# A hybrid RWKV-7 and dilated-attention block: recurrence products with a block-diagonal state, y's gate factors made beside the norm, loads issued ahead, a third staging slot

## The chip, the core and the metric

The kernel runs on one core of one Trainium2 chip, in one launch. The metric is the device time of a run in microseconds (us). TensorE (PE) multiplies, VectorE (DVE), ScalarE (ACT) and GpSimd (POOL) do the element-wise work, SyncE (SP) issues most of the DMAs.

## The reference, cut to what matters

One layer over 1024 tokens with model width 1024, all in float32. The recurrence of 8 heads of 64 and the gated norm behind it are what the change rewrites.

```python
x = x + 0.5 * swiglu(rms_norm(x, ffn1_norm), ffn1_w_gate, ffn1_w_up, ffn1_w_down)   # d_ff 2816
z = rms_norm(x, mix_norm) @ w_in
z_rwkv, z_attn, z_gate = jnp.split(z, [RWKV_COLS, RWKV_COLS + ATTN_COLS], axis=-1)
y_rwkv = rwkv7_time_mix(z_rwkv, ...)
y_attn = dilated_attention_mix(z_attn, cos, sin, q_norm, k_norm)      # 3 groups of 4 heads, rms_norm and rope on q, k
g_rwkv, g_attn = jnp.split(jax.nn.sigmoid(z_gate), 2, axis=-1)
merged = g_rwkv * (y_rwkv @ w_br_rwkv) + g_attn * (y_attn @ w_br_attn)
x = x + merged @ w_out
x = x + 0.5 * swiglu(rms_norm(x, ffn2_norm), ffn2_w_gate, ffn2_w_up, ffn2_w_down)
x = x + jax.nn.sigmoid(rms_norm(x, ple_norm) @ ple_w_gate) * (p_i @ ple_w_proj)
...
# rwkv7_time_mix, per step t and head:
    sa = jnp.einsum('bhvk,bhk->bhv', state, -kk_t)
    state = state * w_t[:, :, None, :] + sa[..., None] * (kk_t * a_t)[:, :, None, :] + v_t[..., None] * k_t[:, :, None, :]
    y_t = jnp.einsum('bhvk,bhk->bhv', state, r_t)
...
    y = (y - mean) * lax.rsqrt(var + GN_EPS)
    y = y * gn_w + gn_b
    y = (y + bonus) * g            # bonus = sum(r k r_k) * v, g = sigmoid(gd) @ g2
```

## The kernel before, in words

The kernel is a chain of stages: FFN1 (0 to 800 us in the profiled execution, with the norm and the first gates behind it), the recurrence (800 to 1403), the attention (1403 to 1750), the merge of the two branches (1750 to 1840), the output product (to 1920), FFN2 (to 2640) and the last gated product. A large product is made of three fp32r matmuls on high and low halves (`mm3`, lines 265 to 267; tile `g` in the stages of interest). Weights are loaded into a ring `wst` of 128x1024 tiles and split by ACT (L249) and POOL (L250) into `wsp`, which `mm3` reads.

In the recurrence the work is cut into 8 units (4 pairs of heads, 2 halves of the sequence), each of 8 chunks of 64 tokens. Three streams, written as generators, run over the units one behind another: A and B prepare a unit (`zstage`, decays, the matrices of a chunk, a triangular solve), and C (`wkv_c`) runs the chunks of a unit, then norms y, gates it, transposes it (L1330) and writes it out. A fourth stream, F, the filler, holds large products that nothing near waits for: the rest of `w_in`, gates, the attention's q, k, v. `weave` fixes the order of all of it when the program is built: each stream yields pairs (busy, wait) in us, and the order is made of them. Afterwards each engine runs its own list strictly in order, so a matmul whose operand is late holds all matmuls behind it, filler too. Filler placed by a long `wait` is what covers a chain.

In a chunk, U = S·QR (L1255, two 64x64 products, one for each head), then DVE makes UV (L1259), then dS = BKn·UV (L1264, two products), then DVE makes the next S (L1265) with ACT's SP = S·decay (L1258). After the chunks of a unit, y's products (L1273, L1279, tile `psy`), then on DVE mean and variance (L1303 to L1315), an rsqrt of eleven small operations (L237 to L243), yc·rs (L1319), on POOL yc·gn_w, +gn_b, the bonus UV·bon and yc+bonus (L1320 to L1325), on DVE yc·gs (L1327, `gsl` is the gate tile loaded from DRAM), and the four transposes. Of the next unit the same queues carry `z`, `kk`, `BK` (L1029, L1031), the products t = QR·BK (L1056) and a matrix N (DVE L1186, read by PE L1192 and L1194).

In the attention, `qk_post` brings q and k of a group (rope, norm, transposes L1516), `attn_core` runs scores (L1576), softmax and output (L1619) over 8 blocks of a group. Three groups follow one another; their filler is the products of the later groups and of the branches (`branch_r`, L1699 loads its gate tiles).

## Time and profile before

| | us |
|---|---|
| median of 3 runs | 2728.99 (2728.43 to 2731.87) |
| profiled execution, time | 2728.36 |
| its span, first to last instruction | 2726.6 |
| PE busy | 2517.1 (92%) |
| DVE busy | 1615.6 (59%) |
| POOL busy | 1144.9 (42%) |
| ACT busy | 972.4 (36%) |
| mean granted clock of TensorE | 0.961 |

Busy time says how full an engine is over the whole span, and nothing of where the others wait for it. PE is the full one; its clock is the share of full speed that was granted while it ran. At a lower clock the same matmul takes longer and counts as longer busy time, so lost time has two forms: idle time of PE, and busy time at a low clock.

### The profile page before, as it was taken

The page shows a single profiled execution, that of the slowest core. Times are in us where ns is not written, and L with a number is a line of the kernel's source. Part 1 is how long each engine was busy: PE and PEld are TensorE (multiplying, and loading weights), DVE is VectorE, ACT ScalarE, POOL GpSimd, SP SyncE. Part 2 cuts the span into 40 slices and gives each one's busy share as a digit, 9 for nine tenths or more (in the row PEclk, how much of TensorE's full clock was granted, in tenths as well). Part 3 has the DMA queues.
Part 4 walks back from the last instruction along what each step waited for, and adds up shares of the span by engine and source line. Part 5 has one row for each costly group of instructions (what it writes and reads, how often), then busy time and mean ns, then how long its engine had stood idle before and what let it go on. Part 6 is the DMA issues. An engine that isn't in the chain of part 4 may idle for free.

```text
span 2726.6 us, 37039 instructions
## 1 busy us (share of the span) xinstructions
PE 2517.1 (92%) x14541; PEld 2037.5 (75%) x14541; DVE 1615.6 (59%) x2519; ACT 972.4 (36%) x1700; POOL 1144.9 (42%) x635
## 2 busy tenths in 40 slices
PE   6899999998999999889988998879889999989899
PEld 5688888777777666667977898658678888868677
DVE  5865556897715555554356326382676565688952
ACT  6433332334434333332224343421533333333541
POOL 2675655554424333332222203151466556553540
PEclk9899999999999999999999999999899999999999
DMA  5222222746333222222231101563032222373532
GB/s 187 93 93 68 88 78 93 263 139 224 117 117 90 53 66 60 56 64 61 74 115 44 63 24 50 174 197 124 31 108 93 79 91 93 125 257 98 177 124 93
DMA packets 272498, 289.18 MB, mean 106 GB/s; under 512 B 46282, under 2 KB 202540, under 8 KB 272068
## 3 DMA queue, kind: packets, MB, share of 16 engines
q1 hardware_dynamic: 264932, 274.59, 30.7%
q10 hardware_dynamic: 7392, 12.23, 1.3%
q8 instruction: 114, 1.87, 0.3%
q14 instruction: 60, 0.49, 0.1%
HBM read 222.64 MB, written 64.14 MB: 105 GB/s over the span
## 4 chain that ended last, share of the span: by engine, by line
PE 47%; DVE 14%; issue 3%; POOL 3%; DMA 2%; ACT 2%; SPq 0%; DVEq 0%; POOLq 0%; ACTq 0%
PE g L265 7%; PE g L267 6%; PE g L266 6%; PE dn L266 5%; PE dn L267 5%; PE dn L265 5%; PE tr L266 1%; PE tr L265 1%; PE tr L267 1%; POOL wsp L250 1%; PE t L1056 1%; PE s L1576 1%; DVE sub L1120 1%; PE pt L1598 1%; PE st L1264 1%
## 5 line engine op out<-in xcount | busy, mean ns | idle before, releaser
L250 POOL TENSOR_TENSOR wsp<-wr,wsp 128x1024 fp32r<-128x1024 f32 (+1 forms) x158 | 355.2, 2254 | 373.8 <-ACT wsp L249 309.0
L250 POOL TENSOR_TENSOR wsp<-wst,wsp 128x1024 fp32r<-128x1024 f32 x71 | 172.9, 2437 | 428.6 <-ACT wsp L249 375.8
L250 POOL TENSOR_TENSOR wsp<-ws,wsp 128x1024 fp32r<-128x1024 f32 x88 | 221.1, 2515 | 212.7 <-ACT wsp L249 210.2
L265 PE MATMUL g<-h,wsp 128*128 128x512 f32 x496 | 221.1, 446 | 15.2 <-DVE h L1715 13.7
L265 PE MATMUL g<-wsp,h 128*128 128x256 f32 (+1 forms) x664 | 217.7, 328 | 13.6 <-ACT raw L1428 10.8
L267 PE MATMUL g<-wsp,h 128*128 128x256 f32 (+1 forms) x664 | 208.2, 314 | 0.0
L266 PE MATMUL g<-wsp,h 128*128 128x256 f32 (+1 forms) x664 | 208.0, 313 | 0.0
L267 PE MATMUL g<-h,wsp 128*128 128x512 f32 x496 | 201.5, 406 | 0.0
L266 PE MATMUL g<-h,wsp 128*128 128x512 f32 x496 | 201.3, 406 | 0.0
L407 DVE TENSOR_TENSOR ws<-wr 128x512 f32<-128x512 f32 x56 | 86.4, 1552 | 161.5 <-POOL x L250 160.1
L249 ACT ACTIVATE wsp<-ws 128x1024 fp32r<-128x1024 f32 (+1 forms) x110 | 106.4, 968 | 202.2 <-PE dn L267 78.0
L249 ACT ACTIVATE wsp<-wr 128x1024 fp32r<-128x1024 f32 (+1 forms) x158 | 134.3, 853 | 121.7 <-PE g L267 46.8
L265 PEld LDWEIGHTS g<-wsp,h 128*128 128x128 f32 x664 | 138.8, 209 | 26.0 <-ACT raw L1428 11.4
L265 PE MATMUL dn<-wsp,h 128*128 128x512 f32 x360 | 143.5, 399 | 12.8 <-DVE x L792 8.8
L266 PE MATMUL dn<-wsp,h 128*128 128x512 f32 x360 | 142.8, 397 | 6.0 <-POOL wsp L250 6.0
L267 PE MATMUL dn<-wsp,h 128*128 128x512 f32 x360 | 142.1, 397 | 0.1
L266 PEld LDWEIGHTS g<-wsp,h 128*128 128x128 f32 x664 | 139.3, 210 | 3.7 <-issue 0.2
L267 PEld LDWEIGHTS g<-wsp,h 128*128 128x128 f32 x664 | 138.8, 209 | 3.8
L265 PEld LDWEIGHTS g<-h,wsp 128*128 128x128 f32 x496 | 96.6, 195 | 46.8 <-DVE h L1715 14.7
L463 DVE TENSOR_TENSOR act<-act,m 128x512 f32<-128x512 f32 x88 | 128.6, 1462 | 1.4
L267 PE MATMUL dn<-h,wsp 128*128 128x512 f32 x320 | 124.7, 390 | 0.0
L266 PE MATMUL dn<-h,wsp 128*128 128x512 f32 x320 | 124.6, 389 | 0.0
(467 smaller groups left out, 6641.8 us busy)
## 6 DMA issues: line engine op xcount, KB each, us to landing
wr<-ffn_w_down SPq DMA_DIRECT2D x44, 1024.0 KB
wst<-w_in SPq DMA_DIRECT2D x60, 512.0 KB
wr<-ffn_w_gate SPq DMA_DIRECT2D x44, 512.0 KB
wr<-ffn_w_up SPq DMA_DIRECT2D x44, 512.0 KB
actD<-act SPq DMA_DIRECT2D x44, 512.0 KB
a<-actD SPq DMA_DIRECT2D x12, 1024.0 KB
gate<-gst SPq DMA_DIRECT2D x26, 256.0 KB
wst<-ffn_w_down SPq DMA_DIRECT2D x10, 512.0 KB
```

Of the source, the lines that this page charges most:

```text
L249: nc.scalar.activation(dst[:, 0], src, AF.Copy)
L250: (lo_eng or nc.vector).tensor_tensor(out=dst[:, 1], in0=src, in1=dst[:, 0].bitcast(F32), op=ALU.subtract)
L265: mm(ps, lhsT=l[0], rhs=r[0], start=first, stop=False)
L266: mm(ps, lhsT=l[0], rhs=r[1], start=False, stop=False)
L267: mm(ps, lhsT=l[1], rhs=r[0], start=False, stop=last)
L407: self.nc.vector.tensor_tensor(out=out, in0=R[:, i], in1=R[:, j], op=op)
L463: eng.tensor_tensor(out=a, in0=a, in1=v, op=ALU.mult)
L1056: PE.matmul(psd[h][:, i2, e].rearrange("p (a s) -> p a s", a=2), lhsT=BK[hr, i, 2 * e:2 * e + 2].rearrange("p a s -> p (a s)"), rhs=QR[hr, ...
L1120: V.tensor_tensor(out=pr[:, :s + 1, :n], in0=XT[:, :s + 1, s:s + 1].to_broadcast([64, s + 1, n]), in1=at[:, s:s + 1, s + 1:].to_broadcast( ...
L1264: PE.matmul(pu[hr, 0, 320:384], lhsT=BKn[:, i, e, hr], rhs=UV[:, i, e, hr], start=True, stop=True)
L1576: PE.matmul(ps[h][:, pr, :nk * P], lhsT=qT[hr, pr, j * P:(j + 1) * P], rhs=kT[hr, pr, k0:k0 + nk * P], start=True, stop=True)
L1598: PE.transpose(pt[:, h], S[:, h, kt * P:(kt + 1) * P], self.ident)
```

## The change

Five edits. (1) The ring `wst` has three slots instead of two. (2) The recurrence keeps a block-diagonal state `Sbd` of 128x128 for each chunk (two persistent tiles, cleared once by POOL): one 128x128 product makes U for both heads, one makes dS, SP is 128x128, and the new S is written by two DVE operations on 64x64 blocks. The chunk's last yield says 0.7 instead of 0.5. (3) POOL makes two factors, `ybv` = (bonus + gn_b)·gs and gs·gn_w, beside the norm; behind the rsqrt DVE alone does yc·rs, yc·gs, yc + ybv, with a yield of 4.0 (`YWAIT`) in between and one of 2.0 before the transposes. (4) `qk_post` issues the raw loads of group 0 ahead and yields longer before its transposes. (5) `branch_r` loads its weights one at a time ahead of their use instead of three at the start, between the gate tiles.

```diff
@@ -40,6 +40,7 @@
 BURST = 2.0
 WIN = 3.0
 ACT = 0.45
+YWAIT = 4.0
 LOW = 0.15
...
@@ -869,6 +870,9 @@
                                     op0=ALU.mult)
         N1 = self.t(sp, [P, 8, 64], "N1")
         nc.gpsimd.memset(N1, 0.0)
+        Sbd = [self.t(sp, [P, 9, P], f"Sbd{q}") for q in range(2)]
+        for q in range(2):
+            nc.gpsimd.memset(Sbd[q], 0.0)
 
         carry = self.t(self.cp, [P, 14], "carry")
...
@@ -1236,41 +1240,38 @@
         for e in range(2):
             A.activation(QR[:, :, 1 - e], psw[e], AF.Copy)
 
-        S = self.t(sp, [P, 9, 64], "S", bufs=2)
+        S = env["Sbd"][u % 2]
         if hf == 0:
             G.memset(S[:, 0], 0.0)
         else:
-            A.activation(S[:, 0], env["Ss"][hb][:, 8], AF.Copy)
-        env["Ss"][hb] = S
+            A.activation(S[:, 0], env["Sbd"][(u - 1) % 2][:, 8], AF.Copy)
         pu = self.t(pp, [P, 2, HALF], "st")
         psy = [pu[:, h, 0:256].rearrange("p (i s) -> p i s", i=4) for h in range(2)]
+        U2, dS = pu[:, 0, 256:384], pu[:, 0, 384:512]
         yield 0, 0.8
         for i in range(4):
             for e in range(2):
-                qs = (1, 0)[e]
                 cc = 2 * i + e
                 pcol = PC[:, cc:cc + 1]
-                for h in range(2):
-                    hr = slice(64 * h, 64 * h + 64)
-                    PE.matmul(pu[ur[e], h, 256:320], lhsT=QR[hr, i, qs], rhs=S[hr, cc], start=True, stop=True)
+                PE.matmul(U2, lhsT=QR[:, i, 0:2].rearrange("p a s -> p (a s)"), rhs=S[:, cc], start=True, stop=True)
                 yield 0.16, 0.5
-                SP = self.t(sp, [P, 64], "SP", bufs=2)
+                SP = self.t(sp, [P, P], "SP", bufs=2)
                 A.activation(SP, S[:, cc], AF.Copy, scale=pcol)
                 V.tensor_tensor(out=UV[ur[e], i, e].rearrange("p (h s) -> p h s", h=2),
                                 in0=Ub[ur[e]].rearrange("p (h i) s -> p h i s", h=2)[:, :, i],
-                                in1=pu[ur[e], :, 256:320], op=ALU.subtract)
+                                in1=U2[ur[e]].rearrange("p (h s) -> p h s", h=2), op=ALU.subtract)
+                PE.matmul(dS, lhsT=BKn[:, i, e], rhs=UV[:, i, e], start=True, stop=True)
                 for h in range(2):
                     hr = slice(64 * h, 64 * h + 64)
-                    PE.matmul(pu[hr, 0, 320:384], lhsT=BKn[:, i, e, hr], rhs=UV[:, i, e, hr], start=True, stop=True)
-                V.scalar_tensor_tensor(out=S[:, cc + 1], in0=pu[:, 0, 320:384], scalar=pcol, in1=SP, op0=ALU.mult,
-                                       op1=ALU.add)
-                yield 0.16, 0.5
+                    V.scalar_tensor_tensor(out=S[hr, cc + 1, hr], in0=dS[hr, hr], scalar=pcol[hr], in1=SP[hr, hr],
+                                           op0=ALU.mult, op1=ALU.add)
+                yield 0.16, 0.7
 
         for i in range(4):
             for h in range(2):
                 hr = slice(64 * h, 64 * h + 64)
                 for e in range(2):
-                    PE.matmul(psy[h][vr[e], i], lhsT=QR[hr, i, (2, 3)[e]], rhs=S[hr, 2 * i + e], start=i == 0, stop=False)
+                    PE.matmul(psy[h][vr[e], i], lhsT=QR[hr, i, (2, 3)[e]], rhs=S[hr, 2 * i + e, hr], start=i == 0, stop=False)
         yield 0.8, 0
         for i in range(4):
             for h in range(2):
...
@@ -1306,6 +1307,14 @@
             V.tensor_tensor(out=hs_(yc)[:, :, h], in0=psy[h], in1=st[:, :, h:h + 1].to_broadcast([P, 4, 64]),
                             op=ALU.subtract)
         env["done"].add(("c0", u))
+
+        bv = self.t(sp, [P, HALF], "ybv")
+        for e in range(2):
+            G.tensor_tensor(out=hs_(bv)[vr[e]], in0=UV[vr[e], :, e].rearrange("p i (h s) -> p i h s", h=2),
+                            in1=bc(bon)[vr[e]], op=ALU.mult)
+        G.tensor_tensor(out=i4(bv), in0=i4(bv), in1=gn[:, 1:2].to_broadcast([P, 4, P]), op=ALU.add)
+        G.tensor_tensor(out=bv, in0=bv, in1=gs, op=ALU.mult)
+        G.tensor_tensor(out=i4(gs), in0=i4(gs), in1=gn[:, 0:1].to_broadcast([P, 4, P]), op=ALU.mult)
         yield 0, 1.5
         sq = self.t(sp, [P, HALF], "ysq")
         A.activation(sq, yc, AF.Square)
...
@@ -1315,16 +1324,12 @@
         V.tensor_scalar(out=var, in0=var, scalar1=1.0 / 64, scalar2=64e-5, op0=ALU.mult, op1=ALU.add)
         yield 0, 1.0
         rs_ = self.rsqrt(sp, var, "grs")
+        yield 0, 3.0
+        V.tensor_tensor(out=hs_(yc), in0=hs_(yc), in1=bc(rs_), op=ALU.mult)
+        yield 0, YWAIT
+        V.tensor_tensor(out=yc, in0=yc, in1=gs, op=ALU.mult)
+        V.tensor_tensor(out=yc, in0=yc, in1=bv, op=ALU.add)
         yield 0, 2.0
-        V.tensor_tensor(out=hs_(yc), in0=hs_(yc), in1=bc(rs_), op=ALU.mult)
-        G.tensor_tensor(out=i4(yc), in0=i4(yc), in1=gn[:, 0:1].to_broadcast([P, 4, P]), op=ALU.mult)
-        G.tensor_tensor(out=i4(yc), in0=i4(yc), in1=gn[:, 1:2].to_broadcast([P, 4, P]), op=ALU.add)
-        for e in range(2):
-            G.tensor_tensor(out=hs_(sq)[vr[e]], in0=UV[vr[e], :, e].rearrange("p i (h s) -> p i h s", h=2),
-                            in1=bc(bon)[vr[e]], op=ALU.mult)
-        G.tensor_tensor(out=yc, in0=yc, in1=sq, op=ALU.add)
-        yield 0, 8.0
-        V.tensor_tensor(out=yc, in0=yc, in1=gs, op=ALU.mult)
         pst = self.t(pp, [P, HALF], "t1", bufs=4)
         for i in range(4):
             PE.transpose(pst[:, i * P:(i + 1) * P], yc[:, i * P:(i + 1) * P], ident)
...
@@ -1480,12 +1485,20 @@
         for g in range(NG):
             yield lambda: g < 2 or ("core", g - 2) in done
             tr = [self.t(sp, [P, 2, T], f"qkT{qk}", bufs=2) for qk in range(2)]
+
+            def load0(n):
+                t = self.t(sp1, [P, T], f"ot{n % 2}").rearrange("p (i h d) -> p i h d", i=4, h=4)
+                nc.sync.dma_start(t.rearrange("p i h d -> p i (h d)"), rawD[n % 2, :, n // 2 * 4:n // 2 * 4 + 4])
+                return t
+
+            if g == 0:
+                r0 = [load0(0), load0(1)]
+                yield 0, 6.0
             for n in range(4):
                 qk, hf = (n % 2, n // 2) if g == 0 else (n // 2, n % 2)
                 Ct, St = self.rt[qk]
                 if g == 0:
-                    raw = self.t(sp1, [P, T], f"ot{n % 2}").rearrange("p (i h d) -> p i h d", i=4, h=4)
-                    nc.sync.dma_start(raw.rearrange("p i h d -> p i (h d)"), rawD[qk, :, hf * 4:hf * 4 + 4])
+                    raw = r0[n]
                 else:
                     yield lambda: (g, qk, hf) in env["raw"]
                     raw = env["raw"][g, qk, hf]
...
@@ -1505,11 +1518,13 @@
                 t2 = self.t(sp, [P, 4, 4, 64], "rt3")
                 V.tensor_tensor(out=t2[:, :, :, 0:32], in0=raw[:, :, :, 32:64], in1=bc(St, 0, 32), op=ALU.mult)
                 V.tensor_tensor(out=t2[:, :, :, 32:64], in0=raw[:, :, :, 0:32], in1=bc(St, 32, 32), op=ALU.mult)
+                if g == 0 and n < 2:
+                    r0.append(load0(n + 2))
                 yield 0, 1.0
                 V.tensor_tensor(out=t1, in0=t1, in1=t2, op=ALU.add)
                 yield 0, 1.0
                 V.tensor_tensor(out=t1, in0=t1, in1=rs[:, :, :, None].to_broadcast([P, 4, 4, 64]), op=ALU.mult)
-                yield 0, 1.6
+                yield 0, 5.0
                 for pr in range(2):
                     ps = self.t(pp, [P, HALF], "pt", bufs=2)
                     for i in range(4):
...
@@ -1684,10 +1699,10 @@
         nc, a = self.nc, self.a
         yield ready
         wc = lambda q: self.wchunk(a["w_br_rwkv"][:, q * 256:(q + 1) * 256].rearrange("(k p) n -> p k n", p=P), 4)
-        W = [wc(q) for q in range(3)]
+        W = [wc(0)]
         yr = []
         for hb in range(4):
-            st = self.t(self.wp, [P, T], "wst", bufs=2)
+            st = self.t(self.wp, [P, T], "wst", bufs=3)
             nc.sync.dma_start(st, yT[hb])
             yr.append([self.half(h2, hb, hf) for hf in range(2)])
             for hf in range(2):
...
@@ -1695,15 +1710,15 @@
         rp = out["rp"] = [[self.t(h2, [P, 2, HALF], f"h{4 + q}{hf}") for hf in range(2)] for q in range(4)]
 
         def tanh(b):
-            t = self.t(self.wp, [P, T], "wst", bufs=2)
+            t = self.t(self.wp, [P, T], "wst", bufs=3)
             nc.sync.dma_start(t, gateD[b])
             return t
 
         th = tanh(0)
         for b in range(KB):
-            if b == 2:
-                W.append(wc(3))
             nxt = tanh(b + 1) if b < KB - 1 else None
+            if b % 2 == 0 and b < 6:
+                W.append(wc(b // 2 + 1))
             w = W[b // 2][:, :, :, (b % 2) * P:(b % 2) * P + P]
             for hf in range(2):
                 hsl = slice(hf * HALF, (hf + 1) * HALF)
```

The other pieces only write `bufs=3` for `bufs=2` for `wst` (in `wchunk`, `forms_1`, `ffn_down` and `slot`), or pass `Sbd` on.

Lines move by one to fifteen: L1056 becomes L1060, L1186 L1190, L1192 L1196, L1194 L1198, L1330 L1335, L265 to L267 become L266 to L268.

First place: PE, where the y of the second unit is transposed, while the next unit is being prepared. `t` are PSUM tiles, `g` are filler products, `yc` is the gated y. Before:

```order
L1183 MATMUL t_1236_7657<-TT_7504,SC_7040 64x32 x4
L265 MATMUL g_7668<-h_790_4903,wsp_7664 128x512
L266 MATMUL g_7668<-h_790_4903,wsp_7664 128x512
L267 MATMUL g_7668<-h_790_4903,wsp_7664 128x512
L1183 MATMUL t_1236_7657<-TT_7504,SC_7040 64x32 x8
L1330 MATMUL t_1241_7689<-cst_p_66,yc_7463 128x128 x4
L1056 MATMUL t_1244_7698<-QR_7600,BK_7601 128x128
L1056 MATMUL t_1245_7699<-QR_7600,BK_7601 128x128
L1192 MATMUL t_1246_7702<-N_882_5609,TT_7504 64x32 x2
L1194 MATMUL t_1246_7702<-TT_7504,N_882_5609 64x32 x2
```

After:

```order
L1187 MATMUL t_1243_7682<-TT_7451,SC_7042 64x32 x8
L1060 MATMUL t_1249_7716<-QR_7624,BK_7625 128x128
L1060 MATMUL t_1250_7717<-QR_7624,BK_7625 128x128
L1060 MATMUL t_1249_7716<-QR_7624,BK_7625 128x128
...
L1196 MATMUL t_1251_7722<-N_882_5609,TT_7451 64x32 x2
L1198 MATMUL t_1251_7722<-TT_7451,N_882_5609 64x32 x2
...
L268 MATMUL g_7693<-h_807_5013,wsp_7689 128x512
L1335 MATMUL t_1252_7769<-cst_p_66,yc_7530 128x128 x4
```

The transposes of `yc` stood ahead of the products of QR and BK; now two pairs of those, 32 products with N and twelve filler matmuls stand ahead of the transposes (the rows left out are one more L1060, products with N, and filler).

Second place: DVE, the same unit, behind the rsqrt. `grsy` is the rsqrt, `gsl` the gate, `ta` and `BK` belong to the next unit. Before:

```order
L1319 TENSOR_TENSOR yc_7463<-yc_7463,grsy_7533 128x512
L889 SCALAR_TENSOR_TENSOR z_1202_7480<-g_7481,omu_5597,zu_7564 128x512
L1017 TENSOR_SCALAR n_1227_7594<-t_1225_7585 128x8
L1018 RECIPROCAL n_1227_7594<-n_1227_7594 128x8
L1327 TENSOR_TENSOR yc_7463<-yc_7463,gsl_7460 128x512
L1015 SCALAR_TENSOR_TENSOR ta_7521<-ta_7521,kk_7550 128x512
L1031 TENSOR_TENSOR BK_7601<-z_1073_6661,iP_7553 128x4x2x64
L1029 SCALAR_TENSOR_TENSOR BK_7601<-ta_7521,iP_7553 128x4x128
L889 SCALAR_TENSOR_TENSOR z_1223_7574<-g_7575,omu_5597,zu_7626 128x512
L1186 TENSOR_TENSOR N_882_5609<-t_1236_7657,cst_r_5592 128x16x16
```

After:

```order
L1328 TENSOR_TENSOR yc_7530<-yc_7530,grsy_7586 128x512
L1019 SCALAR_TENSOR_TENSOR ta_7549<-ta_7549,kk_7564 128x512
L1035 TENSOR_TENSOR BK_7625<-z_1073_6655,iP_7567 128x4x2x64
L1033 SCALAR_TENSOR_TENSOR BK_7625<-ta_7549,iP_7567 128x4x128
L1330 TENSOR_TENSOR yc_7530<-yc_7530,gsl_7527 128x512
L1331 TENSOR_TENSOR yc_7530<-yc_7530,ybv_7536 128x512
L893 SCALAR_TENSOR_TENSOR z_1230_7604<-g_7605,omu_5597,zu_7651 128x512
L1190 TENSOR_TENSOR N_882_5609<-t_1243_7682,cst_r_5592 128x16x16
```

The product with the gate stood ahead of `ta` and `BK`; now both gating operations stand behind `BK` and ahead of the one that writes N.

Third place: POOL, the factors of the same unit. Before, from the bonus to the next unit's `kk`:

```order
L1323 TENSOR_TENSOR ysq_7497<-UV_6607,bon_6621 64x512 x2
L1030 TENSOR_TENSOR QR_7600<-z_1090_6752,sg_7518 128x4x128
L987 MEMSET sg_8171 128x8
L1320 TENSOR_TENSOR yc_7463<-yc_7463,gn_5792 128x512
L1321 TENSOR_TENSOR yc_7463<-yc_7463,gn_5792 128x512
L1325 TENSOR_TENSOR yc_7463<-yc_7463,ysq_7497 128x512
L250 TENSOR_TENSOR wsp_7815<-wst_7813,wsp_7815 128x1024
L885 MEMSET zu_7626 128x1
L1013 TENSOR_TENSOR z_1073_6661<-z_1073_6661,tmpa_7590 128x512
L1106 TENSOR_TENSOR kk_7550<-z_1090_6752,z_1073_6661 128x512
```

After:

```order
L1110 TENSOR_TENSOR kk_6900<-z_1004_6210,z_991_6150 128x512
L1313 TENSOR_TENSOR ybv_7536<-UV_6609,bon_6623 64x512 x2
L1315 TENSOR_TENSOR ybv_7536<-ybv_7536,gn_5796 128x512
L1316 TENSOR_TENSOR ybv_7536<-ybv_7536,gsl_7527 128x512
L1317 TENSOR_TENSOR gsl_7527<-gsl_7527,gn_5796 128x512
L1222 MEMSET N_882_5609 128x8x16
L251 TENSOR_TENSOR wsp_7475<-wst_7473,wsp_7475 128x1024
L1137 MEMSET TT_7451 128x1024
...
L1034 TENSOR_TENSOR QR_7624<-z_1089_6734,sg_7546 128x4x128
...
L1017 TENSOR_TENSOR z_1073_6655<-z_1073_6655,tmpa_7614 128x512
L889 MEMSET zu_7651 128x1
L1110 TENSOR_TENSOR kk_7564<-z_1089_6734,z_1073_6655 128x512
```

The three operations on `yc` stood among QR, z and `kk` of the next unit; the factors now stand right behind the preceding unit's `kk`, ahead of the clearing of N, and nothing of y stands between QR and `kk`.

Counted over the whole list, 120 more filler matmuls of 512 columns stand ahead of the last transposes of y than before, and as many fewer behind them; group 0's attention core has 14 filler matmuls of 512 columns and 38 of 256 between its scores and its end, where before it had 168 and 34. Their total in the program is unchanged.

## Rows read from the trace of the kernel before

**Rows 1.** The page's busy times: us, share, instructions of each engine.
```profile
PE 2517.1 (92%) x14541; PEld 2037.5 (75%) x14541; DVE 1615.6 (59%) x2519; ACT 972.4 (36%) x1700; POOL 1144.9 (42%) x635
```

**Rows 2.** Waits of PE, 800 to 1400: in total, times, longest, us.
```profile
PE t L1330 <- DVE yc L1327: 22.7, 6, 7.4
PE t L1056 <- ACT wsp L249: 6.2, 2, 3.3
...
PE t L1056 <- DVE BK L1029: 2.9, 2, 2.2
```

**Rows 3.** Windows: length, busy us (count) of PE, PEld, DVE, ACT, POOL; PEclk, DMA, GB/s.
```profile
860.00:1300.00 440.00, 397.53 (x3878) 291.84 (x3878) 243.19 (x584) 135.65 (x277) 143.72 (x120) 0.92 0.23 61
...
1150.00:1160.00 10.00, 6.46 (x38) 4.80 (x38) 5.47 (x6) 3.99 (x8) 5.59 (x4) 0.50 0.42 116
...
1300.00:1400.00 100.00, 100.00 (x1143) 88.08 (x1142) 37.66 (x114) 28.71 (x62) 27.81 (x20) 1.00 0.25 74
```

**Rows 4.** Timeline of PE from the second unit's y products: start, us, [idle before].
```profile
990.17 1.15 PE L1279 MATMUL st<-UV,SC 128*64 128x64 f32 x32
...
1011.88 0.63 PE L1330 MATMUL t<-cst_p,yc 128*128 128x128 f32 x4 [2.97 <-DVE yc L1327]
...
1015.84 1.21 PE L1056 MATMUL t<-QR,BK 64*128 64x128 f32 x4 [3.33 <-ACT wsp L249]
```

**Rows 5.** Timeline of POOL, same stretch.
```profile
1004.89 1.27 POOL L1320 TENSOR_TENSOR yc<-yc,gn 128x512 f32<-128x512 f32 x1 [1.02 <-DVE yc L1319]
...
1007.61 1.28 POOL L1325 TENSOR_TENSOR yc<-yc,ysq 128x512 f32<-128x512 f32 x1
```

**Rows 6.** Timeline of DVE, same stretch.
```profile
994.26 0.74 DVE L1303 TENSOR_REDUCE gst<-st 128x4 f32<-128x256 f32 x2
...
1004.12 0.69 DVE L1319 TENSOR_TENSOR yc<-yc,grsy 128x512 f32<-128x512 f32 x1
...
1008.92 2.82 DVE L1327 TENSOR_TENSOR yc<-yc,gsl 128x512 f32<-128x512 f32 x1 [3.13 <-POOL yc L1325]
...
1013.94 1.75 DVE L1029 SCALAR_TENSOR_TENSOR BK<-ta,iP 128x512 f32<-128x512 f32 x1
...
1016.27 0.41 DVE L1186 TENSOR_TENSOR N<-t,cst_r 128x256 f32<-128x256 f32 x1
```

**Rows 7.** Groups by form, 800 to 1400: busy us, mean ns of one, idle before.
```profile
L1056 PE MATMUL t<-QR,BK 64*128 64x128 f32 x256 | 27.6, 318 | 9.3 <-ACT wsp L249 6.2 <-DVE BK L1029 2.9 <-ACT Qn L1160 0.2
...
L1265 DVE SCALAR_TENSOR_TENSOR S<-st,PC,SP 128x64 f32<-128x64 f32 x64 | 18.1, 282 | 43.0 <-PE st L1264 43.0
```

**Rows 8.** Timeline of PE in one chunk.
```profile
984.91 0.33 PE L1255 MATMUL st<-S,QR 64*64 64x64 f32 x4
985.17 0.50 PE L265 MATMUL g<-h,wsp 128*128 128x512 f32 x1
985.51 0.39 PE L266 MATMUL g<-h,wsp 128*128 128x512 f32 x1
985.74 0.40 PE L267 MATMUL g<-h,wsp 128*128 128x512 f32 x1
```

**Rows 9.** Waits of PE, 1400 to 1920.
```profile
PE g L265 <- DVE h L1715: 13.7, 2, 12.1
...
PE pt L1516 <- DVE rt L1511: 8.2, 2, 5.3
```

**Rows 10.** Timeline of PE in the attention, from y's last transposes to group 0's end.
```profile
1402.80 0.63 PE L1330 MATMUL t<-cst_p,yc 128*128 128x128 f32 x4 [1.56 <-DVE yc L1327]
...
1499.46 0.91 PE L1576 MATMUL s<-qkT,qkT 64*128 64x256 f32 x5
...
1505.81 1.14 PE L1576 MATMUL s<-qkT,qkT 64*128 64x256 f32 x8
...
1513.70 1.10 PE L1619 MATMUL po<-PT,vt 128*64 128x128 f32 x14
```

**Rows 11.** Chain that ended last, in the merge: start, us, what.
```profile
1768.05 6.22 DMA wst<-gate
```

14 lines of the change are left out of this document (7 added, 7 removed).

## The prediction

> **What bounds the kernel now.** I read the page's busy times first: TensorE is busy for 2517.1 of 2726.6 us [rows 1]. So it bounds the kernel nearly everywhere, and an edit can gain only its idle time, its time at a low clock, or matmul time. Then the windows, to see where these lie: from 1300 to 1400 PE has no gap and the full clock, while from 860 to 1300 it is busy for 397.5 of 440 us at a clock of 0.92 [rows 3]. That is 42.5 us idle. The clock costs at most 397.5 × 0.08 = 32 us; I take 25, an estimate, since in the low slices part of the busy time is latency of small matmuls and not their rate. The two belong together: the slice at 1150, behind such a gap, is a third idle and at 0.50, which is the lower of the clock's two levels [rows 3]. Then the waits, to see what made the gaps: the transposes of y waited for DVE 22.7 us in 6 waits, and the products of QR and BK behind them 9.1 us (6.2 + 2.9) [rows 2]. ACT is named for the 6.2, but there the wait is BK's, as the timelines show: BK ends at 1015.69 (1013.94 + 1.75) [rows 6], and L1056 begins at 1015.84 [rows 4].
>
> The timeline of one unit tells why. The y products end at 991.32 (990.17 + 1.15); PE then has filler and the next unit's work until 1008.91, when it stops for the transposes (1011.88 − 2.97) [rows 4]. That is 17.6 us of work. The chain to the gated y takes longer: its reduction begins only at 994.26, since DVE was still on the next unit's triangular solve; yc·rs is done at 1004.81; POOL's three operations and handoffs take it to 1008.89 [rows 5]; the gate multiply, 2.82 us, ends at 1011.74 [rows 6]. So 20.4 us of chain stand against 17.6 us of cover. In the queue of DVE the next unit's `ta` and BK stand behind that multiply, so PE stops a second time, 3.33 us, four microseconds on [rows 4].
>
> **The change, part by part.**
>
> *y's gate.* POOL's three operations leave the chain: from yc·rs to the multiply they took 4.1 us (1004.81 to 1008.92) [rows 5, 6]. DVE gets one operation more. Of the two behind the rsqrt each costs between 0.69 and 2.82 us, which are the same size of operation alone and beside POOL [rows 6]; I take 1.5. In the order the next unit's solve is finished before the y products, which gives the chain up to 2.9 us (991.32 to 994.26). So y is ready some 5 us earlier against its products. On PE two pairs of BK products, 32 with N and three more filler matmuls stand ahead of the transposes: about 4.5 us more cover. The 2.8 us that the chain lacked are more than made up: the 22.7 us go.
>
> What is late next is BK, then N. BK no longer stands behind the gate multiply (2.82 us) nor its wait (3.13) [rows 6], so it is ready about 5 us earlier; PE asks for it about 2 us earlier, nine filler matmuls having left the place ahead of it. The 9.1 us shrink to 2 or 3. N now stands on DVE behind both gate operations, and everything on PE behind L1196 waits for it: before, N ended 1.0 us after BK (1015.69 to 1016.68); now 1.5 + 1.5 for the gate, 0.7 for one operation of z (taken as the 0.69 of yc·rs) and 0.41, some 4 us after [rows 6]. BK gains more than that, so I charge 0.5 us for each unit, 4 in all; the bound is 3 us, 24 in all. POOL's factors stand ahead of work that before followed `kk` directly, but need only v, the bonus and the gate; 5 operations of about 1.3 us [rows 5] lie in POOL's idle time.
>
> In 860 to 1300 I thus expect the idle time to fall from 42.5 to about 15.5: **−27**. The clock falls behind the gaps and is full where there are none [rows 3]; with 4 us of gap in place of 32 near the y transposes, some 16 of the 25 us come back: **−16** (bounds −5 and −22).
>
> *The products of a chunk.* Two products of a pair take one slot: from L1255's start to the filler behind it 0.26 us pass, against 0.23 from one filler matmul to the next [rows 8]. One 128x128 product in float32 has no row. The nearest is L1056, 128 columns with 64 rows: 27.6 us for 256 records, 108 ns for one [rows 7], two records for a product, 0.22 us. So a place costs 0.22 instead of 0.26 if 64 rows and 128 take the same time, −0.04; from above 0.1 more than now, if each switch exposes something. For 128 places the bounds are −5 and +13; I take **0**. The Trainium skill's page "TensorEngine Tiling (Array Packing)", section "Overview", speaks against the edit: small tiles run side by side, up to twice as fast where a dimension is at most 64, and one full product gives that up. By it the sum would be that of the third rival; no row here has such a full product, so the trace does not yet show it. DVE's second update, 64 × 0.28 us = 18 us [rows 7], and SP of double width lengthen a chunk's loop by about 0.3 us; three more filler matmuls in each chunk (0.7 us) cover that. Without cover it would cost 64 × 0.3 = 19 us.
>
> *Filler moved.* The longer yields put 120 filler matmuls ahead of the last transposes, 120 × 0.23 = 27.6 us. They lengthen the recurrence and shorten what follows; no sum, unless they are missed there.
>
> *Attention.* From the last transposes to group 0's last output pass 112.0 us (1402.80 to 1514.80), most of them filler. One block of the core takes 6.35 us (1499.46 to 1505.81) [rows 10]. Now about 39 us of PE work stand before the scores (by the order 192 filler matmuls of 256 columns and 43 of 512, taken at half and the whole of 0.23 us, and 7 us of transposes), then 8 × 6.35 = 51 us of nearly bare core and some 6 us of tail: 96 us, 16 less. By its end 18 us of filler less are left than before, counted from the program's start. So 16 + 18 are saved against 27.6 moved in: −6; group 2 finds its q and k later relative to its filler, +1 (bounds 0 and +10). The 8.2 us for `rt` [rows 9] are inside these numbers. I take **−5** (bounds −15 and +15).
>
> *Merge, third slot.* The gate tile came 6.22 us after the weight split that freed its slot [rows 11], and PE waited 13.7 us for what was made of the gates [rows 9]. With three slots two gates are issued early; but the last weights now come late and may cost 3.8. Net **−3** (bounds −8 and +2). In FFN the third slot hides nothing that now waits: 0 to −3, taken as 0. The two clearings of `Sbd` lie beside FFN products.
>
> The sum: −27 − 16 + 0 − 5 − 3 = −51. The profiled execution took 2728.36 us, 0.6 below the median: 2677 for it, **2678** for the median.
>
> **The rivals.**
>
> 1. *The stall moves to N or half remains.* If N comes 3 us late in each unit, the 24 us are a new gap where the old was 32, and the clock stays low with it: −27 + 20 and −16 + 11, with −8 outside, gives −20: **2709**. For it speaks that N has two operations ahead of it that run 2.82 us when POOL is at work [rows 6]; against it that POOL has less to do there.
> 2. *The bare attention core.* A block holds 3.2 us of PE work (1.14 + 1.10 [rows 10] and about as much of transposes). With no filler beside it the clock may fall; at 0.6 the block takes 2.1 us more, 8 × 2.1 = 17 us, and if a third of the 27.6 us moved then finds no gap to be missed from, 10 more: −51 + 17 + 10 = −24: **2705**. For it speaks that the order leaves 14 filler matmuls of 512 columns there; against it that the clock held 0.92 through the gaps of the recurrence [rows 3].
> 3. *The full products take twice the place.* If the two products of a pair run side by side now and the full one gains nothing from its width, a place goes from 0.26 to 0.52 us [rows 8]: 128 × 0.26 = 33 us more, −18 in all: **2711**. Against it stands L1056's 108 ns for 128 columns [rows 7]. This is the case that the tiling page's rule describes.
> 4. *Slower: POOL's five operations delay BK.* They are issued before the next unit's QR, z and `kk`. If the gate tile comes late, POOL stands, and BK with it: five operations of 1.3 us are 6.5 us. Each microsecond of such a gap costs about another 0.8 at the clock (25 against 32 before). With 6.5 us in 8 units 52 + 42 = 94 stand in place of 32 + 25 = 57: +37, less the 8 outside, +29: **2758**. It decides from 57 / (8 × 1.8) = 4.0 us of gap for a unit. Against it: POOL idles for most of that stretch.
>
> **How the numbers follow.** The forecast has 0.55, the first three rivals 0.11, 0.11 and 0.07, the fourth 0.09; 0.04 is for a gain beyond 2645, 0.03 for no effect. The likeliest one's own range is 2652 to 2700: at best −27 − 22 − 5 − 15 − 8 = −77, at worst N's 20 and the products' 13 are added to some part. The whole range adds at the lower end a halving of the 15.5 us of idle time left, and above the first three rivals and some of what they give together: 2645 to 2722. It leaves out the fourth, the case of no effect, half of the best one and the rivals in combination.
>
> About 0.2% of the time, 5.5 us, is what a measurement of this kernel can tell from no change. Faster than that are the forecast, the first three rivals and the best case, 0.55 + 0.29 + 0.04 = 0.88. I take 0.06 off, since two rivals together reach no change or pass it: half goes to each side. So faster 0.82, same 0.03 + 0.03 = 0.06, slower 0.09 + 0.03 = 0.12.
>
> **What would show it.** Right: L1335's wait for yc under 5 us in all, no gap above 1 us at L1060 and L1196 in most units, a clock of 0.97 or more from 860 to 1300, a chunk's product at 0.2 to 0.3 us. The last transposes come at about 1402.8 − 43 + 27.6 = 1387, the end of group 0 some 16 us nearer to them. Wrong: a row of waits of PE for N (L1190) or BK of over 20 us; U2 and dS at 0.5 us a piece; low clock in the attention's core; PE waiting for S in the chunks.

## The result, and the profile after

The changed kernel takes 2694.07 us (median of 4 runs, 2689.59 to 2697.53) against 2730.43 for the kernel before; the ratio is 0.9865, with a 95% interval of 0.9853 to 0.9878. That is 36 us less, where the forecast was 51 less. The profiled execution took 2694.29 us, with a span of 2692.5.

The page of the changed kernel, the busy times and the granted clock in 40 slices:

```profile
PE 2492.6 (93%) x14285; PEld 2040.2 (76%) x14285; DVE 1623.3 (60%) x2591; ACT 977.2 (36%) x1700; POOL 1142.7 (42%) x637
...
PEclk9899999999999999999997999889899999999999
```

TensorE is busy for 24.5 us less than before [rows 1]; busy time at a low clock is in that, and so is matmul time that the change removed. The windows of the changed kernel (length, busy us and count of PE, PEld, DVE, ACT, POOL, then PEclk):

```profile
860.00:1300.00 440.00, 407.62 (x4112) 330.62 (x4108) 263.88 (x683) 150.83 (x302) 149.91 (x126) 0.97 0.26 70
...
1425.00:1475.00 50.00, 45.10 (x233) 30.25 (x231) 34.86 (x113) 20.93 (x64) 10.12 (x5) 0.74 0.11 33
1720.00:1770.00 50.00, 30.25 (x99) 22.71 (x99) 30.94 (x33) 7.36 (x10) 15.25 (x7) 0.74 0.71 204
```

From 860 to 1300 the clock rose from 0.92 to 0.97 and PE is busy for 10 us more [rows 3]. The two lower rows show where it fell: over the whole of group 0's attention core, from its first scores to its statistics, the clock is 0.77 (1427.3 to 1486.4), where it was 0.95 before (1442.9 to 1512.3); over the merge it is 0.80, where it was 0.89. The waits of TensorE of the changed kernel, 800 to 1400:

```profile
PE st L1256 <- DVE Sbd L1266: 9.8, 7, 2.1
PE st L1263 <- DVE UV L1260: 6.7, 9, 2.3
PE t L1060 <- ACT Qn L1164: 3.4, 1, 3.4
...
PE t L1196 <- issue: 3.0, 4, 1.0
...
PE t L1196 <- ACT zu L891: 1.6, 1, 1.6
PE t L1060 <- DVE BK L1033: 1.5, 3, 0.6
```

The wait of the transposes for y, 22.7 us [rows 2], is gone and has no row at all; BK is down to 1.5 with 0.2 for its other half, and N's place (L1196) to 4.6 us in all. At the head stand two that are 16.5 us together: inside the chunks U's product waits for the state and dS's product for UV. Before they were 4.6 us:

```profile
PE st L1264 <- DVE UV L1259: 2.9, 2, 1.6
...
PE st L1255 <- DVE S L1265: 1.7, 1, 1.7
```

By stage, from the start of the last instruction of a line in the two traces:

| | before | after | difference |
|---|---|---|---|
| last transposes of y | 1403.2 | 1378.8 | −24.4 |
| end of group 2's statistics | 1749.0 | 1698.7 | −50.3 |
| last gate product of the merge | 1843.4 | 1801.8 | −41.6 |
| end of the span | 2726.6 | 2692.5 | −34.1 |

With the 27.6 us of filler that the new order puts ahead of the transposes (the prediction's estimate), 52 us are gained up to there and the attention lost 2; the merge lost 9, and what follows it 7.5. Of the 52, 3 lie ahead of the recurrence, whose first products of QR and BK start at 842.3 before and at 839.3 after.

### The profile page after: what moved, and what is told of

It reads as the page before. It is cut to its first block, busy times and chain, and to the rows that moved or that the text cites. A ratio compares the mean times of both kernels' runs of the same rounds, so it can differ in the third digit from the quotient of the medians.

```text
span 2692.5 us, 36600 instructions
## 1 busy us (share of the span) xinstructions
PE 2492.6 (93%) x14285; PEld 2040.2 (76%) x14285; DVE 1623.3 (60%) x2591; ACT 977.2 (36%) x1700; POOL 1142.7 (42%) x637
## 4 chain that ended last, share of the span: by engine, by line
PE 46%; DVE 12%; issue 4%; POOL 3%; DMA 3%; ACT 2%; SPq 0%; DVEq 0%; POOLq 0%; ACTq 0%
PE g L266 7%; PE g L268 6%; PE g L267 6%; PE dn L267 5%; PE dn L268 5%; PE dn L266 5%; POOL wsp L251 2%; PE tr L268 1%; PE tr L267 1%; PE tr L266 1%; DVE X L1126 1%; DVE sub L1124 1%; PE s L1591 1%; PE t L1060 1%; DMA wr<-ffn_w_down 1%
## 5 line engine op out<-in xcount | busy, mean ns | idle before, releaser
L266 PE MATMUL g<-wsp,h 128*128 128x256 f32 (+1 forms) x664 | 213.9, 322 | 19.5 <-ACT raw L1433 9.8
L266 PE MATMUL g<-h,wsp 128*128 128x512 f32 x496 | 215.9, 435 | 13.6 <-DVE h L1730 8.6
L268 PE MATMUL g<-wsp,h 128*128 128x256 f32 (+1 forms) x664 | 207.1, 312 | 0.0
L267 PE MATMUL g<-wsp,h 128*128 128x256 f32 (+1 forms) x664 | 206.0, 310 | 0.7 <-POOL wsp L251 0.7
L268 PE MATMUL g<-h,wsp 128*128 128x512 f32 x496 | 200.6, 405 | 2.1 <-POOL wsp L251 2.1
L267 PE MATMUL g<-h,wsp 128*128 128x512 f32 x496 | 200.6, 404 | 0.0
L266 PEld LDWEIGHTS g<-wsp,h 128*128 128x128 f32 x664 | 137.0, 206 | 29.6 <-ACT raw L1433 10.7
L266 PE MATMUL dn<-wsp,h 128*128 128x512 f32 x360 | 144.3, 402 | 6.5 <-DVE x L793 6.4
L267 PE MATMUL dn<-wsp,h 128*128 128x512 f32 x360 | 144.0, 400 | 6.5 <-POOL wsp L251 6.5
L268 PE MATMUL dn<-wsp,h 128*128 128x512 f32 x360 | 143.1, 399 | 0.8 <-DVE h L251 0.6
L267 PEld LDWEIGHTS g<-wsp,h 128*128 128x128 f32 x664 | 136.9, 206 | 4.9 <-POOL wsp L251 0.9
L268 PEld LDWEIGHTS g<-wsp,h 128*128 128x128 f32 x664 | 136.9, 206 | 4.6 <-issue 1.0
L266 PEld LDWEIGHTS g<-h,wsp 128*128 128x128 f32 x496 | 96.4, 194 | 38.5 <-DVE h L1730 9.5
L268 PE MATMUL dn<-h,wsp 128*128 128x512 f32 x320 | 124.6, 389 | 0.0
L266 PE MATMUL dn<-h,wsp 128*128 128x512 f32 x320 | 124.5, 389 | 0.0
```

What stands on the lines that cost most here:

```text
L266: mm(ps, lhsT=l[0], rhs=r[0], start=first, stop=False)
L267: mm(ps, lhsT=l[0], rhs=r[1], start=False, stop=False)
L268: mm(ps, lhsT=l[1], rhs=r[0], start=False, stop=last)
```

## Experiments

All are ratios to the kernel before, with 95% intervals. Every experiment changes one thing in the kernel before or in the changed kernel. The kernel before was timed again with each set, and its medians lie between 2727.24 and 2731.43 us, so differences below are taken from the ratios.

**The products.** The first run takes the full products out of the change.

```diff
-                PE.matmul(U2, lhsT=QR[:, i, 0:2].rearrange("p a s -> p (a s)"), rhs=S[:, cc], start=True, stop=True)
+                for h in range(2):
+                    hr = slice(64 * h, 64 * h + 64)
+                    PE.matmul(pu[ur[e], h, 256:320], lhsT=QR[hr, i, qs], rhs=S[hr, cc], start=True, stop=True)
...
```

The product dS, SP and the update follow in the same way; the yield stays at 0.7.

> The changed kernel with the recurrence's products as before: two 64x64 products for U and two for dS, the state of 64 columns, one update on VectorE; every yield as in the change, so the filler stands where the change has it. Theory: a full product takes 0.14 us of TensorE where it does not wait (984.38 to 984.52 in the profile after) against 0.26 us for a pair, so taking it away costs 128 x 0.12 = 15 us, less some of the 16.5 us that TensorE now waits for the two updates and UV: 2700 to 2710 us. Rival, the pair was free beside the waits and the gain lies in the y chain and the yields alone: 2694 or, with one update less on VectorE, down to 2685.

Measured: 0.9945 (0.9931 to 0.9959), 2718.04 us. Against the change's 0.9865 the small products cost 0.8%, some 22 us: more than expected, and of the sign of the first theory. The timelines of PE show where. Of the change, one chunk:

```profile
984.15 0.40 PE L268 MATMUL g<-h,wsp 128*128 128x512 f32 x1
984.38 0.38 PE L1256 MATMUL st<-Sbd,QR 128*128 128x128 f32 x2
984.52 0.48 PE L266 MATMUL g<-h,wsp 128*128 128x512 f32 x1
984.84 0.40 PE L267 MATMUL g<-h,wsp 128*128 128x512 f32 x1
```

Of the run with small products:

```profile
986.43 0.40 PE L268 MATMUL g<-h,wsp 128*128 128x512 f32 x1
986.75 0.33 PE L1256 MATMUL st<-S,QR 64*64 64x64 f32 x4
987.01 0.50 PE L266 MATMUL g<-h,wsp 128*128 128x512 f32 x1
987.35 0.39 PE L267 MATMUL g<-h,wsp 128*128 128x512 f32 x1
```

A full product holds its place for 0.14 us (984.38 to 984.52), a pair for 0.26. The filler matmul ahead takes 0.23 us ahead of a full product (984.15 to 984.38) and 0.32 ahead of a pair (986.43 to 986.75), and the one behind 0.32 and 0.34. Over all chunks of the two traces I get means, for the pair and then for the full product, of 0.26 and 0.18 us for the place, 0.33 and 0.28 for the filler ahead, 0.31 and 0.30 behind: 128 × (0.08 + 0.05 + 0.01) = 18 us. The rest balances: by slices of ten us the run with small products is idle for 7.0 us less than the change and loses 10.3 us more to the clock (25.6 and 19.5 from 860 to 1410, against 32.6 and 9.2 from 860 to 1380). The Trainium skill's page "TensorEngine Tiling (Array Packing)", section "Tiling Modes", says that a change of tiling mode drains TensorE. The longer filler ahead of a pair, 0.32 against 0.23, is in keeping with that, but no run separates a drain from the two more records of a pair. The doubling that the section "Overview" led one to expect did not come.

Then the products alone in the kernel before, once with the chunk's yield of 0.7 as here, and once without the last line pair, so with 0.5:

```diff
+        Sbd = [self.t(sp, [P, 9, P], f"Sbd{q}") for q in range(2)]
...
-                yield 0.16, 0.5
+                yield 0.16, 0.7
```

> The kernel before with the block-diagonal state, the full products and the yield of 0.7 in the chunk alone; y's chain, the loads and the two slots as before. Theory: 15 us from the products, and the 24 more filler matmuls in a unit's chunks let the next unit's solve end before the y products, which takes up to 2.9 of the chain, so part of the 22.7 us wait for y goes too: 2700 to 2712 us. Rival, products free: 2720 to 2730.

> The kernel before with the block-diagonal state and the full products alone, the chunk's last yield left at 0.5, so that the order of the filler is that of before. Theory: the products save 128 x 0.24 us = 31 (0.12 in their own place, 0.09 in the filler matmul ahead of each, 0.03 in the one behind), less some 10 of waits in the chunk; what made the run with the yield of 0.7 slower than before was filler taken from y's cover and the attention: 2705 to 2715 us. Rival, the longer loop costs what the products save whatever the yield: 2725 to 2735.

Measured: 1.0024 (1.0015 to 1.0034) and 1.0036 (1.0022 to 1.0050). Both are slower than before, and both theories that I set on them fell: the saving of matmul time does not show, and it was not the longer yield that ate it. The waits of TensorE of the run with 0.5, 800 to 1400, where the filler stands as in the kernel before:

```profile
PE t L1330 <- DVE yc L1327: 37.0, 6, 7.9
PE st L1262 <- DVE UV L1259: 7.1, 4, 2.0
...
PE st L1255 <- DVE Sbd L1265: 3.7, 3, 1.7
```

The wait for y grew from 22.7 [rows 2] to 37.0 us, and the chunks wait too. Summed over slices of ten us (860 to 1400), PE is idle for 58.1 us against 42.5, and busy time times the missing share of the clock is 35.6 against 25.4: 26 us worse, against some 16 us that its shorter places give by the same means. That leaves 10 us, most of the 12.4 by which this trace comes later to y's last transposes (1415.6 against 1403.2). The trace is that of the slowest of six executions, 17 us above the one of before; the ratio makes it 10. In the run with 0.7 the wait for y is down to 13.9 us, so that part of its theory held, but BK and Qn take 18.6 and the chunks 15.6 in its place. What TensorE saves ahead of y's transposes it gives back at waits for VectorE, as long as that chain comes last.

**y's chain.** The gate factors and yields alone in the kernel before, and the change without them:

```diff
-        yield 0, 8.0
-        V.tensor_tensor(out=yc, in0=yc, in1=gs, op=ALU.mult)
+        yield 0, YWAIT
+        V.tensor_tensor(out=yc, in0=yc, in1=gs, op=ALU.mult)
+        V.tensor_tensor(out=yc, in0=yc, in1=bv, op=ALU.add)
...
```

> The kernel before with the gate factors made on GpSimd beside the norm and the new yields behind the rsqrt, nothing else of the change. Theory: the wait for y (22.7 us), most of that for BK (9.1) and some 10 of the clock go: 2690 to 2702 us. Rival, the gain needs the longer chunk loop that moves the solve away: 2710 to 2725.

> The changed kernel with y's gate as before (GpSimd's operations behind the rsqrt, yields of 2.0 and 8.0), all else as changed. Theory: y's chain is worth 25 to 35 us by itself, 2715 to 2730 us. Rival, the chunk's loop with its longer yield has already taken the wait away: under 2705.

Measured: 0.9923 (0.9909 to 0.9937) alone, 2709.57 us, between the two expectations and nearer to the rival's; and 1.0063 (1.0050 to 1.0077), 2749.19 us, for the change without it, 19 us above the expected range. So y's chain is worth 0.8% alone and 2.0% within the change. Alone it already takes the wait for y away: the trace of that run has no such row from 800 to 1400, so the rival fell in its mechanism. What it does not bring is the clock. By slices (860 to 1380) PE is idle for 25.9 us, 16.6 less than before, but loses 21.5 to the clock, only 3.9 less; BK still costs 5.7 us. The waits of the change without y's part, 800 to 1420:

```profile
PE t L1332 <- DVE yc L1329: 13.9, 5, 4.9
PE t L1060 <- DVE BK L1033: 9.2, 6, 2.9
...
PE t L1060 <- ACT Qn L1164: 7.0, 2, 4.3
...
PE t L1060 <- DVE BK L1035: 2.8, 1, 2.8
```

The wait for y is back in part, BK's two halves are 12.0 us where the change has 1.7, and Qn's is 7.0 where it has 3.4; by slices of ten us (860 to 1430) PE is idle for 54.9 us and loses 33.9 to the clock.

**The chunk's yield.** The change with 0.5 in place of 0.7:

```diff
-                yield 0.16, 0.7
+                yield 0.16, 0.5
```

> The change with the chunk's last yield at 0.5 again: by the order 123 filler matmuls of 512 columns move from the recurrence back into the attention, all of them between the first scores and the end of group 0's core (14 becomes 137). Theory: the core of group 0 ran bare at a clock of 0.74 (1425 to 1475) and the filler moved ahead was not given back, so the stage gains 10 to 20 us; the chunks then wait longer for the second update and UV than the 16.5 us of now, 5 to 10 more: 2680 to 2692 us. Rival, the longer yield is needed for the chunk's longer loop: each chunk waits 0.3 us more, 64 x 0.3 = 19 and the clock with it, 2700 to 2715.

Measured: 0.9924 (0.9908 to 0.9940), 16 us slower than the change. My theory fell; the rival's size is right and its reason is not, for the chunks waited less than in the change (7.0 for UV and 3.7 for the update, against 6.7 and 9.8). By slices of ten us (860 to 1370) PE is idle for 32.9 us, as in the change (32.6 from 860 to 1380), but 21.7 us are lost to the clock against 9.2. The full product's place also has a mean of 0.21 us here and 0.18 in the change, some 4 us over 128. The trace is of the slowest of six executions, 9 us above their median. One unit of it shows a place:

```profile
1060.23 1.15 PE L1280 MATMUL st<-UV,SC 128*64 128x64 f32 x32
...
1078.47 0.46 PE L1060 MATMUL t<-QR,BK 64*128 64x128 f32 x2 [1.76 <-DVE BK L1033]
1079.76 1.22 PE L1060 MATMUL t<-QR,BK 64*128 64x128 f32 x6 [0.83 <-ACT Qn L1164]
```

BK is late by 1.76 us, Qn by 0.83 more, and the products behind run slow: six records of L1060 take 1.22 us at a granted clock of 0.50, the lower of its two levels, where eight of them take 0.72 at 1.00 ten microseconds later, at 1088.93. From the last transposes to group 2's statistics this run takes 343.3 us; less the 123 × 0.23 = 28.3 us of filler given back that is 315.0, against 319.9 in the change. So the attention gained 5 us, and not the 10 to 20 that I hoped for. BK comes late there in part because of GpSimd: the operation that writes it ran for 2.84 us in this unit, beside a weight split, and for 1.77 in the same one of the change, where no split lies beside it.

```profile
1074.97 2.80 POOL L251 TENSOR_TENSOR wsp<-wst,wsp 128x1024 fp32r<-128x1024 f32 x1
```

```profile
1075.48 2.84 DVE L1033 SCALAR_TENSOR_TENSOR BK<-ta,iP 128x512 f32<-128x512 f32 x1
```

The rest of the 1.76 us is not traced.

**The attention's loads and yields.**

```diff
-            if g == 0:
-                r0 = [load0(0), load0(1)]
-                yield 0, 6.0
...
-                yield 0, 5.0
+                yield 0, 1.6
```

> The change with group 0's raw loads and yields as before. By the order 34 filler matmuls of 512 and 34 of 256 columns then stand in the core and not ahead of it (14 becomes 48, 38 becomes 60). Theory: in the core they cover idle time and clock, ahead of it they only fill while rope is made, where TensorE then waits some 8 us more for rt: 2690 to 2698 us, no change. Rival, the raw loads ahead shorten the way to the scores: 2700 to 2708 without them.

Measured: 0.9908 (0.9891 to 0.9924), 12 us slower than the change: the rival. From the last transposes to group 2's end this run takes 326.8 us (1386.0 to 1712.8), the change 319.9. That is 7 of the 12 us; the rest lies, in this trace, ahead of the transposes, where nothing was edited. I had put this edit at a few microseconds. A bare core does lose clock in the change (0.77 above), but more filler in the core did not win it back.

**The merge.** Where the change lost 9 us. The order of SyncE decides when the merge's gate tile `wr` is asked for. Before, it is asked for 14.8 us behind group 2's statistics, ahead of the `fb` loads; in the change 48.4 us behind them, and behind those loads:

```profile
1763.77 0.46 SPq L1745 DMA_DIRECT2D wr<-gate  x1
...
1768.48 1.27 SPq L1671 DMA_DIRECT2D fb<-f  x2
```

```profile
1745.81 1.23 SPq L1686 DMA_DIRECT2D fb<-f  x2
1747.09 0.59 SPq L1760 DMA_DIRECT2D wr<-gate  x1
```

The first variant has the branch's weights as before (the last two pieces), the second issues both gate tiles behind the `w_br_attn` loads (the first piece), the third has the weights as before and the first tile ahead:

```diff
+        g0 = [gate_tile(0, 0), gate_tile(0, 4)]
...
-        W = [wc(0)]
+        W = [wc(q) for q in range(3)]
...
-                W.append(wc(b // 2 + 1))
+                W.append(wc(3))
```

> The change with the branch product's loads in the order of before (three weights at the start, the fourth in the middle), three slots kept. By the order the merge's gate tile then stands ahead of the fb loads in SyncE's list, eight rows earlier. Theory: the 10.3 us that TensorE waited for the merge's gate tile and the 2.1 for the late weight go, and with the third slot no gate tile of the branch is late: 2680 to 2688 us. Rival, three weights at the start and fewer gates ahead bring back the wait of 12 us for the branch's gate tile: 2692 to 2698.

> The change with the merge's first two gate tiles issued by SyncE right behind the last w_br_attn load, eleven rows ahead of where they stood. Theory: the wait of 10.3 us for the merge's gate goes, most of it stays gained: 2683 to 2688 us. Rival, the 2 MB ahead of the fb and branch gate loads make those late instead (9.8 us for fb as it is): 2692 to 2700.

> The change with the branch's loads in the order of before, three slots, and the merge's first gate tile issued behind the last w_br_attn load. Theory: the two late tiles of the merge are both early then, 10 to 14 us less than the change: 2680 to 2685 us. Rival, the merge is bound by its transfers in sum, and a tile ahead makes another late: 2688 to 2696.

Measured: 0.9863 (0.9841 to 0.9884), 0.9842 (0.9822 to 0.9863) and 0.9852 (0.9837 to 0.9866). None is clear of the change's 0.9865. The waits of TensorE, 1700 to 1802, of the change, of the run with the weights as before, and of the run with both gate tiles ahead:

```profile
PE g L266 <- DVE wr L1766: 19.5, 5, 10.3
PE g L266 <- DVE h L1730: 8.6, 2, 5.4
```

```profile
PE g L266 <- DVE wr L1766: 9.8, 4, 3.5
PE g L266 <- DVE h L1730: 5.1, 2, 2.7
```

```profile
PE g L266 <- DVE h L1730: 10.9, 1, 10.9
PE g L266 <- DVE wr L1772: 8.6, 7, 2.6
```

With the weights as before both waits fall. With both gate tiles ahead the wait for the merge's gate falls from 19.5 to 8.6 and its longest from 10.3 to 2.6, while the one for the branch's gate rises from 8.6 to 10.9, now in one piece. From group 2's statistics to the last gate product the three variants take 88.4, 96.3 and 91.5 us in their traces, the change 103.1 and the kernel before 94.4. So in these traces the order of loads costs the merge what the table shows; that winning it back shortens the whole program is not shown, since the ratios do not part. The fastest median of the study, 2684.24 us, is that of both gate tiles ahead, but its interval overlaps that of the change, so it is not shown to beat it.

**The third slot.**

```diff
-        st = self.t(self.wp, [P, 1024], "wst", bufs=3)
+        st = self.t(self.wp, [P, 1024], "wst", bufs=2)
```

> The change with two slots in the staging ring instead of three. Theory: the third slot hides little, since the late tile of the merge is the one in the other ring: 2690 to 2698 us, no change. Rival, the gate tiles of the branch and the late weights then wait for a slot, 6 to 8 us each, two or three times: 2702 to 2715.

Measured: 0.9886 (0.9873 to 0.9899), 2696.29 us, within the theory's range. The ratios differ by 0.0021, some 6 us, and the intervals overlap: the slot may be worth anything from nothing to some 11 us.

**The waits in the chunk.** One update over the whole tile (the blocks off the diagonal then mix the two heads of a pair):

```diff
-                for h in range(2):
-                    hr = slice(64 * h, 64 * h + 64)
-                    V.scalar_tensor_tensor(out=S[hr, cc + 1, hr], in0=dS[hr, hr], scalar=pcol[hr], in1=SP[hr, hr],
-                                           op0=ALU.mult, op1=ALU.add)
+                V.scalar_tensor_tensor(out=S[:, cc + 1], in0=dS, scalar=pcol, in1=SP, op0=ALU.mult, op1=ALU.add)
```

> The change with one update of the state over the whole 128x128 tile instead of two over its diagonal blocks; the blocks off the diagonal, which mix the two heads of a pair, are then not kept at zero, so the state is another. Theory: half of the 16.5 us for which TensorE waits in the chunks (9.8 for the update, 6.7 for UV) comes from the second update on VectorE: 8 us and some clock less, 2682 to 2688 us. Rival, the waits come from the solve's long operations ahead on VectorE: 2692 to 2697.

Measured: 0.9861 (0.9849 to 0.9874), 2690.12 us, between the two ranges; by the ratio no change, as the rival said. The wait for the update falls from 9.8 to 4.9 us and that for UV rises from 6.7 to 8.8: 13.7 us together, so the second update has a part of 3 us. What makes the long ones is seen in the change itself. VectorE, GpSimd and TensorE at the longest of these waits, a timeline each:

```profile
979.04 0.22 DVE L1124 TENSOR_TENSOR sub<-X,at 64x63 f32<-64x63 f32 x1
979.29 2.27 DVE L1126 TENSOR_TENSOR X<-X,sub 64x63 f32<-64x63 f32 x1
981.59 0.21 DVE L1124 TENSOR_TENSOR sub<-X,at 64x60 f32<-64x60 f32 x1
...
982.33 0.28 DVE L1260 TENSOR_TENSOR UV<-Ub,st 64x128 f32<-64x128 f32 x1
```

```profile
979.12 2.36 POOL L251 TENSOR_TENSOR wsp<-wst,wsp 128x1024 fp32r<-128x1024 f32 x1 [14.03 <-ACT wsp L250]
```

```profile
982.66 0.49 PE L1263 MATMUL st<-UV,BKn 128*128 128x128 f32 x2 [2.31 <-DVE UV L1260]
```

An operation of the solve that takes 0.22 us elsewhere takes 2.27, from just behind the start of GpSimd's weight split to its end (979.12 + 2.36); UV stands behind it, and TensorE waits 2.31 us. All seven waits in the chunks of 1.4 us or more, 12.6 of the 16.5 us, have such an operation of over 2 us on VectorE ahead of them, which ends within 0.1 us of a split's end. No run moves the splits, so this is read from timelines alone. And the splits were there before, when the chunks waited 4.6 us: with the yield of 0.7 and small products they wait 9.3, with full products and 0.5 they wait 10.7, with both 16.5. So the new order and the full products each add to the waits at these splits; in which way is not shown.

## Why the prediction was right, and where it was not

The sign, the size within its range and the place were right: 36 us less against 51, 2694 in a range of 2645 to 2722. Its steps:

- **y's wait goes: right.** 22.7 us became none. The product of QR and BK waits 5.1 us where it waited 9.3 (BK 1.7, and once 3.4 for Qn), and N's place has 4.6 where I charged 4; its five waits end 0.1 us after N is written. The first rival (N) and the fourth (BK behind POOL's factors) fell. Run by itself the edit gives 21 us, within the change 54.
- **Idle time −27: the size failed.** By slices of ten us it fell from 42.5 to 32.6, −10. The places of y, BK and N went from 32.0 to 9.7 us, about as forecast. The step "three more filler matmuls in each chunk cover that" was the one that failed: the chunks' waits went from 4.6 to 16.5 us. The second update, which I charged, makes some 3 of them; the long ones are VectorE standing still under GpSimd's splits.
- **Clock −16: the number came, its reason only in part.** 25.4 us became 9.2. But I put all of it down to y's gap, and the two runs that close that gap with small products lose 21.5 (y's chain alone) and 19.5 (the change without full products): −4 and −6. The rest came only together with the full products, by a way that no run shows. It also scatters: four runs that leave the recurrence as it is in the change (those that change only the attention's loads, the branch's weights or the merge's gate tiles) lose 10.3 to 16.1 by the same sum, so that the −16 is the best of five.
- **Products 0, bounds −5 and +13: mis-sized.** They give some 18 us in the places by the means, 22 by the time of the whole program. I worked out 0.22 us for a place from L1056's 108 ns a record, which is a mean over records at either level of the clock and of products of 64 rows; the full product measures 0.14 at best and 0.18 in the mean. And I counted only the place, not the filler matmul ahead, 0.05 us longer in the mean beside a pair. The third rival, double the place, had the sign wrong. It pays only where y is out of the way: alone the edit is slower than before.
- **Attention −5: failed as a size, +2.** Group 0's last output came 110.5 us behind the first of the last transposes, against 112.0 before: 1.5 nearer, and not 16. Of the 96 us that I allowed for it, the failed step is the "39 us of PE work" ahead of the scores. TensorE was busy for 37.2 us there, but the stretch took 48.5, since I left out its waits, 11.3 us, of which one is 9.4:

```profile
1387.55 5.67 POOL L1512 TENSOR_TENSOR rt<-ot,rope 128x1024 f32<-128x1024 f32 x2 [13.69 <-DMA ot<-raw]
```

```profile
1391.10 3.21 DVE L1524 TENSOR_TENSOR rt<-rt,rt 128x1024 f32<-128x1024 f32 x1
```

```profile
1400.14 1.06 ACT L1510 ACTIVATE rt<-ot 128x1024 f32<-128x1024 f32 x1 [10.21 <-DVE ass L1513]
```

```profile
1401.52 0.58 PE L266 MATMUL g<-wsp,h 128*128 128x256 f32 x1 [9.36 <-ACT raw L1433]
```

The filler waits for ACT's copy of its product, ACT has in its own list a square for group 0's norm ahead of it, and that waits for VectorE, whose rope operations take 2.71 to 3.21 us beside GpSimd's (0.68 and 1.23 just behind). The second rival was right in its sign: the core loses clock, and with its tail took 61.7 us where I had 57. By slices 14.7 us are lost to the clock from 1380 to 1490, against 7.1 before from 1400 to 1510. But the two runs that put filler back there, by the chunk's yield and by the loads as before, were slower by 16 and 12 us in all.
- **Merge −3: wrong sign, +9.** I looked at the branch's gate tiles and the late weight, and not at what the same edit does to the merge's own gate tile, which SyncE now issues behind the `ob` and `fb` loads: 10.3 us in one wait.
- **FFN2 and the last product 0: +7.5 between the traces, from the merge's end on.** FFN2's first products (2004 to 2379 before) take the same time; the loss comes in pieces of 0.6 to 3 us ahead of them and behind. The stretch takes 883 to 893 us over all traces here, and the changed kernel's executions spread over 8 us; this one stays open.

Of the forecast's −51, idle and clock gave 26 instead of 43, the products 18 that were not in it, and the stages behind cost 18 where they were to give 8. The sum of the measured terms in the recurrence, 10 + 16 + 18 = 44, and the 3 ahead of it are 5 short of the 52 in the table; that rest I could not place.

So the mechanism at y was right, and the nearness of the total is partly luck: a gain that stood at 0 made up for what the other terms missed. Without the full products the kernel takes 2718.04 us, outside the likeliest range of 2652 to 2700 and only just within the whole one. Of the signs of being wrong two came, low clock in the attention's core and PE waiting for the state in the chunks; of the signs of being right, y's wait and the clock of 0.97 came, a product of 0.2 to 0.3 us and group 0's end 16 us nearer did not.

## What to carry to other kernels

A saving on the busiest engine counts only behind whatever it waits for: here the full products are worth 22 us in the changed kernel, where y's chain is short, and cost 10 us alone, while it is long. Added one by one they would have been dropped; taken out of the whole one by one, they show their worth. And where an edit rewrites the order of loads, look in the issuing queue for every tile of that queue, also those that the edit doesn't name.
